# A two-layer expert kernel: early buffers for the first gather, context rows inside expert 0, the last two experts combined on chip

## The chip, the cores and the metric

The kernel runs on one core of a Trainium2 chip. The metric is the device time of one execution in microseconds (us). Comparisons are made between runs on the same chip; the profile is one execution, recorded instruction by instruction.

The engines go by short names: PE (TensorE, matrix products), DVE (VectorE), ACT (ScalarE), POOL (GpSimd) and SP (SyncE, which issues most of the DMA transfers). POOL issues the indirect transfers (gather and scatter by row numbers). All transfers share 16 DMA engines.

## The reference

512 latent tokens and 128 context tokens of width 1024 go through two layers with shared weights. All numbers are 32-bit floats. Each layer is:

```
h   = x * (1 + scale1) + shift1
mix = [windowed attention | neighbourhood attention | retention](h @ w_in) @ w_out
x   = layernorm(alpha * x + gate1 * mix)
h   = x * (1 + scale2) + shift2
aff = softmax(h @ w_router)                      # 16 experts
gate, idx = top_k(aff.T, cap)                    # each expert picks its tokens: 64 latent, 16 context
y_e = (silu(h[idx] @ w_gate) * (h[idx] @ w_up)) @ w_down * gate
ff  = scatter-add of the y_e of all experts to their tokens
x   = layernorm(alpha * x + gate2 * ff)
```

Latent and context tokens choose separately. So each expert works on 80 rows, and reads 8 MB of gate and up weights and 4 MB of down weights for them.

## The kernel before, in words

**Memory.** SBUF is handed out in 25 slots of 128 x 2048 floats (`Slots`), some cut into two halves (`Halves`). A 1 MB weight tile fills one slot. `ahead` is a list of all weight tiles in the order of use; `ahead.fill(n, keep)` issues loads as long as more than `keep` slots are free in the order of the program. A load into a slot whose last user still runs waits for it. Instructions are put in order on each engine by a planner, from costs that it assumes and from the order of the program; `tc.issue_after(x)` adds that an instruction stands behind `x` on its engine.

**From the mixer to the experts (`mixer`).** The output projection runs in two halves of 512 columns over five tiles of 128 tokens (tiles 0 to 3 latent, 4 context). Beside it `router(t)` computes the affinities of a tile and stores the normalized rows to DRAM (`znd`). Then `topk` (L1330 and following) finds the 64 best latent tokens of each expert in rounds of eight on DVE, merging two halves; `picked` (L1553) is the cast of the latent row numbers. After it on DVE come the gated output, the router and the top-k of the context tile (L1556 to L1566).

**The experts (`moe`).** `gather(0)` fetches the first expert's latent rows and context rows in two transfers, `gather(e)` the others two experts ahead, into three buffers `xgb`. `first_x` turns expert 0's rows with PE; `turned_x` and `turned_act` turn the other rows and the activations on DVE in 32 x 32 pieces (L1611). In `gate_up` the latent rows are the stationary operand, four column groups at a time (`lat`, L1681), and the context rows follow (`cxt`, L1685). For expert 0 all eight tiles run their latent products first, then all context products, and only these give the tiles' slots back. `down(e-1)` comes after `gate_up(e)`. It scales the result (L1739, L1746) and adds it to `acc` in DRAM by a scatter on POOL (L1754). `init` (L1455 to L1457) computes the start values of `acc`, `z * (alpha g) + alpha b`, on DVE and stores them.

**The end of a layer.** Expert 15's result isn't scattered. The sums are loaded from `acc` (L1814) after expert 14's scatter, and `combine` adds them up in PSUM: identity times sums (L1832, L1834) plus a 0/1 matrix times the result in two parts, high and low (L1835, L1836). `ln2` normalizes (L608, L1882) and, in layer 1, scales and shifts (L1884, L1885) and stores; in layer 0 it loads the tables and first weights of layer 1 after the sums, and starts layer 1's first projection.

Lines of the code that the steps turn on:

```
hf.hold = True
xgb = [hf.get(F32, "xg") for _ in range(3)]
xgs = [gather(0)]
init(6, g_last[0])
...
yh, yl = down(NE - 1, turned_act(prev))
for t in range(NT):
    sums = nc.sync.dma_start(accs[t], acc[l][128 * t:128 * t + 128])
```

## Time and profile before

| what | us |
|---|---|
| median of 3 runs (lowest to highest) | 1949.7 (1946.35 to 1953.62) |
| the profiled execution | 1953.35 |
| its span, first to last instruction | 1951.6 |
| PE busy | 1807.9 (93%) |
| DVE busy | 1151.8 (59%) |
| ACT busy | 417.7 (21%) |
| POOL busy | 224.5 (12%) |

The two expert passes take 440 to 964 us and 1390 to 1913 us of the span. PE is busy in nearly all of both, but a busy PE is not a PE at its peak: matmuls overlap, and their clock has two levels, 1.2 and 2.4 GHz. The granted clock is given as a share of the higher one.

### The profile page before, as it was taken

The page shows a single profiled execution, that of the slowest core. Times are in us where ns is not written, and L with a number is a line of the kernel's source. Part 1 is how long each engine was busy: PE and PEld are TensorE (multiplying, and loading weights), DVE is VectorE, ACT ScalarE, POOL GpSimd, SP SyncE. Part 2 cuts the span into 40 slices and gives each one's busy share as a digit, 9 for nine tenths or more (in the row PEclk, how much of TensorE's full clock was granted, in tenths as well). Part 3 has the DMA queues.
Part 4 walks back from the last instruction along what each step waited for, and adds up shares of the span by engine and source line. Part 5 has one row for each costly group of instructions (what it writes and reads, how often), then busy time and mean ns, then how long its engine had stood idle before and what let it go on. Part 6 is the DMA issues. An engine that isn't in the chain of part 4 may idle for free. (4 is left out here: it accounts for less than half of the span.)

```text
span 1951.6 us, 34372 instructions
## 1 busy us (share of the span) xinstructions
PE 1807.9 (93%) x14135; PEld 903.2 (46%) x14135; DVE 1151.8 (59%) x2966; ACT 417.7 (21%) x886; POOL 224.5 (12%) x176
## 2 busy tenths in 40 slices
PE   6999999868999999989879999989699999998995
PEld 3766767752333333323357667878223333332322
DVE  3654547568556585636386554675884657655356
ACT  2354533111000000000054654322100000000001
POOL 3200002101000110000062000130100101000003
PEclk9999999878999999999989999999699999999997
DMA  9343554488999999999545342247799999999973
GB/s 367 114 147 132 190 166 167 137 304 302 400 392 406 391 397 386 408 416 409 210 157 188 130 145 99 86 159 251 272 398 400 404 392 394 400 392 408 409 315 136
DMA packets 95980, 555.00 MB, mean 284 GB/s; under 512 B 13850, under 2 KB 18864, under 8 KB 36432
## 3 DMA queue, kind: packets, MB, share of 16 engines
q1 hardware_dynamic: 89104, 528.27, 68.9%
q0 software_dynamic: 6720, 24.54, 5.0%
q8 instruction: 111, 1.82, 0.4%
q14 instruction: 45, 0.37, 0.1%
HBM read 526.07 MB, written 26.70 MB: 283 GB/s over the span
## 5 line engine op out<-in xcount | busy, mean ns | idle before, releaser
L1681 PE MATMUL pA<-w,xT 128*32 128x512 f32 x4096 | 494.9, 605 | 24.3 <-DVE xT L1628 11.7
L1681 PEld LDWEIGHTS pA<-w,xT 128*32 128x32 f32 x4096 | 134.3, 112 | 340.6 <-issue 301.0
L1685 PE MATMUL pA<-w,xT 128*32 128x512 f32 x2048 | 270.0, 603 | 3.0 <-DVE xT L1652 3.0
L1681 PE MATMUL pB<-w,aT 128*32 128x512 f32 x2048 | 246.6, 598 | 5.7 <-issue 5.6
L1611 DVE STREAM_TRANSPOSE aT<-z 32x128 f32<-32x128 f32 x432 | 130.2, 301 | 53.2 <-PE pB L1681 27.6
L1681 PEld LDWEIGHTS pB<-w,aT 128*32 128x32 f32 x2048 | 69.9, 111 | 161.5 <-issue 146.6
L1685 PEld LDWEIGHTS pA<-w,xT 128*32 128x32 f32 x2048 | 68.1, 112 | 158.9 <-issue 153.3
L1685 PE MATMUL pB<-w,aT 128*32 128x512 f32 x1024 | 133.3, 593 | 0.0
L1611 DVE STREAM_TRANSPOSE aT<-turn 32x128 f32<-32x128 f32 x336 | 101.4, 302 | 25.3 <-PE pB L1681 19.4
L1715 DVE TENSOR_TENSOR z<-z,pA 128x512 f32<-128x512 f32 x18 | 12.4, 688 | 174.7 <-PE pA L1681 139.9
L348 PE MATMUL pA<-hhi,wh 128*128 128x512 f32 x224 | 92.1, 411 | 0.0
L1713 ACT ACTIVATE z<-pA 128x512 f32<-128x512 f32 x18 | 10.8, 598 | 376.6 <-PE pA L1681 376.6
L350 PE MATMUL pA<-hhi,wl 128*128 128x512 f32 x224 | 88.3, 396 | 0.5 <-DVE wl L345 0.5
L349 PE MATMUL pA<-hlo,wh 128*128 128x512 f32 x224 | 88.3, 394 | 0.0
L1685 PEld LDWEIGHTS pB<-w,aT 128*32 128x32 f32 x1024 | 35.6, 111 | 76.8 <-issue 75.0
L345 DVE TENSOR_TENSOR wl<-w,wh 128x1024 fp32r<-128x1024 f32 (+2 forms) x46 | 57.6, 1286 | 21.9 <-ACT wh L344 14.3
L348 PE MATMUL pA<-wh,cs 128*128 128x512 f32 x160 | 68.1, 428 | 1.9 <-ACT cs L344 1.9
L1713 ACT ACTIVATE turn<-pA 128x512 f32<-128x512 f32 x14 | 8.4, 597 | 274.3 <-PE pA L1681 274.3
L344 ACT ACTIVATE wh<-w 128x1024 fp32r<-128x1024 f32 (+2 forms) x50 | 53.8, 1121 | 51.9 <-DMA w<-win 29.3
L350 PE MATMUL pA<-wh,cs 128*128 128x512 f32 x160 | 64.2, 405 | 0.0
L349 PE MATMUL pA<-wl,cs 128*128 128x512 f32 x160 | 64.1, 401 | 0.0
L1754 POOL DMA_INDIRECT acc<-z,idx x16 | 23.5, 1466 | 343.6 <-DVE z L1746 326.8
(517 smaller groups left out, 2948.5 us busy)
## 6 DMA issues: line engine op xcount, KB each, us to landing
w<-wgu SPq DMA_DIRECT2D x256, 1024.0 KB, 19.9
w<-wdn SPq DMA_DIRECT2D x124, 1024.0 KB, 21.4
wada<-wada SPq DMA_DIRECT2D x48, 1024.0 KB, 5.0
w<-win SPq DMA_DIRECT2D x20, 1024.0 KB, 7.1
w<-wout SPq DMA_DIRECT2D x8, 1024.0 KB, 4.8
znd<-z SPq DMA_DIRECT2D x8, 512.0 KB
w<-wdn POOLq DMA_DIRECT2D x4, 1024.0 KB, 5.6
acc<-z SPq DMA_DIRECT2D x8, 512.0 KB, 3.3
```

Source lines behind the costliest of these rows:

```text
L344: hi_op[:] = [S.activation(hi[s], src[s], AF.Copy)]
L345: lo_op[:] = [E.tensor_tensor(lo[s], src[s], f32(hi[s]), op=ALU.subtract)]
L348: T.matmul(out, lh, rh, start=first, stop=False)
L349: T.matmul(out, lh, rl, start=False, stop=False)
L350: T.matmul(out, ll, rh, start=False, stop=last)
L1611: V.transpose(out, rows.rearrange("p (k q f) -> p k q f", q=4, f=32)[:, :, q, :])
L1681: T.matmul(p[32 * g:32 * g + 32], x[:, 64 * ko + 32 * i:64 * ko + 32 * i + 32], w[:, 512 * n:512 * n + 512], start=(ko == 0), stop=(ko == 7))
L1685: T.matmul(p[32 * g:32 * g + 32], x[:, 512 + 32 * ko:544 + 32 * ko], w, start=first, stop=last)
L1713: S.activation(act[:, 0:512], pl[0], AF.Silu)
L1715: V.tensor_mul(act[:, 0:512], act[:, 0:512], pl[1])
L1754: G.indirect_dma_start(out=acc[l], out_offset=IndirectOffsetOnAxis(ap=idx[:, e:e + 1], axis=0), in_=y[0:CAP, 0:1024], in_offset=None, comp ...
```

## The change

Six things change.

1. Expert 0's buffers (`early`: the turned rows and the three gather buffers) are taken and cleared in the mixer, before the second half of the output projection. The gather of the latent rows is issued behind `picked`; the context tile's top-k and places are put behind the latent part of `first_x` on DVE (`ctx_places`), and its rows are turned before the eighth latent tile of expert 0 instead of after it.
2. The `acc` start values of tiles 0 and 1 are computed on POOL before the top-k, those of tiles 2 to 4 on DVE after expert 0's activation. The rows `alpha g`, `alpha b` are loaded one tile later and scaled after the router of tile 3.
3. `kept_busy(22)`: 22 products of 256 columns with the identity on PE behind the output projection, whose result nobody reads.
4. Experts 14 and 15 are both kept on chip (`on_chip`), stacked in 128 rows for the latent tokens and 64 for the context tokens; the 0/1 matrix grows to match. Expert 15's activation is turned into a buffer of its own, before expert 14's down.
5. The sums are loaded right behind the last weights and one weight tile of the next layer; the first weight split of the next layer and the identity products of two tiles' sums stand before the last result.
6. `KQ` goes from 5 to 2 (free slots kept back from the weights up to expert 13), `NQ` from 2 to 0 (weight loads issued on POOL's queue).

```diff
-NQ = 2
+NQ = 0
-IW = 1
+IW = 2
-KQ = 5
+KQ = 2
...
+        def init(ts, E, after=None):
+            for i, op in ((0, ALU.mult), (1, ALU.add)):
+                for t in ts:
+                    z = zs[t]
+                    if after is not None:
+                        with tc.issue_after(after):
+                            E.tensor_tensor(z, z, agb[0][:, 1024 * i:1024 * i + 1024], op=op)
+                    else:
+                        E.tensor_tensor(z, z, agb[0][:, 1024 * i:1024 * i + 1024], op=op)
+                    if i:
+                        st(acc[l][128 * t:128 * t + 128], z)
+                        hf.free(z)
+            if NT - 1 in ts:
+                sl.free(*agb)
...
+        def scale_rows():
+            with tc.issue_after(e_last[0]):
+                for i in range(2):
+                    S.activation(agb[0][:, 1024 * i:1024 * i + 1024], agb[0][:, 1024 * i:1024 * i + 1024], AF.Copy,
+                                 scale=ALPHA)
+        def kept_busy(n):
+            p = psA()
+            with tc.issue_after(o_last[0]):
+                for _ in range(n):
+                    T.matmul(p[:, 0:256], ident, cst[:, 0:256], start=True, stop=True)
...
+        early = sl.get(F32, "xT"), [hf.get(F32, "xg") for _ in range(3)]
...
         drain(run_all(PY, o=ctx_out(), z=router(3)))
+        scale_rows()
+        kept_busy(22)
...
         ahead.fill(99, KO)
+        init((0, 1), G)
         topk(affT[:, 0:256], affT2, CAPL, cand[:, 0], cand[:, 1], cst[0:32, C_OFF:C_OFF + 1])
...
+        def ctx_places(after):
+            with tc.issue_after(after):
+                topk(affT[0:16, 256:384], affT2[0:16, 0:128], CAPC, selc[0:16, 0, 0:CAPC], selc[0:16, 1, 0:CAPC],
+                     float(NLAT))
+                for x in (1, 0):
+                    V.transpose(gsel[64:96, x, :], selc[:, x, :])
+                V.tensor_copy(idxC, gsel[CAPL:CAP, 1, 0:16])
+                V.tensor_copy(idx[CAPL:CAP], gsel[CAPL:CAP, 1, 0:16])
...
+                if e == 0 and ko == 7:
+                    next(first)
                 for q in range(2):
                     lat(pl[q], xT, w[:, 1024 * q:1024 * q + 1024], ko)
...
+            with tc.issue_after(x_last[2] if e else t_last[0]):
+                act_mul[:] = [V.tensor_mul(act[:, 0:512], act[:, 0:512], pl[1]).ins]
...
+        def on_chip(i, e, pl, pc, y):
+            if i == 0:
+                for x in "LC":
+                    yk[x] = hf.get(F32R, "yh"), hf.get(F32R, "yl")
+            o, q = slice(64 * i, 64 * i + 64), slice(32 * i, 32 * i + 32)
+            (Lh, Ll), (Ch, Cl) = yk["L"], yk["C"]
+            for n in range(2):
+                r, c = slice(64 * n, 64 * n + 64), slice(512 * n, 512 * n + 512)
+                st_ = lambda: V.scalar_tensor_tensor(y[o, c], pl[r], gateL[r, e:e + 1], g2[r, 0:512],
+                                                     op0=ALU.mult, op1=ALU.mult)
+                with tc.issue_after((lo_op[0] if i and l + 1 < DEPTH else sq_last[0]).ins):
+                    st_()
+                S.activation(Lh[o, c], y[o, c], AF.Copy)
+            for n in range(2):
+                c = slice(512 * n, 512 * n + 512)
+                lo = V.tensor_tensor(Ll[o, c], y[o, c], f32(Lh[o, c]), op=ALU.subtract)
...
-        xgs = [gather(0)]
-        init(6, g_last[0])
+        first_gather(slice(0, CAPL), znd[l][0:NLAT], idx)
+        xgs = [xgb[0]]
...
         xT, prev = next(first), None
+        ctx_places(x_last[1])
+        first_gather(slice(CAPL, CAP), znd[l], idxC)
...
-            init(7, x_last[1])
+            if e == 0:
+                init((2, 3, 4), V, act_mul[0])
+            if e == NE - 1:
+                left = len(ahead.todo)
+                if l + 1 < DEPTH:
+                    ahead_layer(l + 1)
+                rest = ahead.todo[left + 1:]
+                del ahead.todo[left + 1:]
+                ahead.fill(99, 3)
+                hf.free(*xgb)
+                accs.extend([hf.get(F32, "acc") for _ in range(NT)])
+                for t in range(NT):
+                    sums = nc.sync.dma_start(accs[t], acc[l][128 * t:128 * t + 128])
+                last_aT = turned_act(act, hf.get(F32, "aT"))
...
+        with tc.issue_after(sums.ins):
+            ahead.fill(KF, 4)
+            if l + 1 < DEPTH:
+                ahead.have.insert(0, ahead.have.pop(4))
+                first_ws[l + 1] = first_w(l + 1)
+            down(NE - 1, last_aT)
...
+        begin(0)
+        begin(1)
         return combine, sums.ins
```

`begin(t)` issues a tile's identity products, and `combine(t)` the two others.

## Rows read from the trace of the kernel before

**Rows 1.** Stretches of pass 1: length, busy per engine (instructions), PE clock, DMA share, GB/s.

```profile
1370.00:1380.00 10.00, 2.56 (x12) 2.30 (x12) 9.16 (x35) 1.12 (x2) 0.29 (x1) 0.50 0.97 404
1380.00:1390.00 10.00, 3.95 (x22) 3.68 (x21) 5.91 (x30) 2.42 (x7) 2.12 (x4) 0.50 0.53 184
1390.00:1400.00 10.00, 9.82 (x68) 2.51 (x72) 9.55 (x12) 0.58 (x2) 3.44 (x3) 0.73 0.28 74
1400.00:1410.00 10.00, 8.50 (x80) 2.62 (x76) 7.03 (x11) 2.90 (x6) 0.90 (x1) 0.95 0.95 358
...
1430.00:1790.00 360.00, 360.00 (x3360) 109.01 (x3356) 221.13 (x551) 27.75 (x47) 27.68 (x21) 1.00 1.02 399
...
1880.00:1910.00 30.00, 27.18 (x237) 8.95 (x232) 12.29 (x31) 2.38 (x4) 0.99 (x1) 0.94 0.38 152
```

**Rows 2.** Timeline of PE: start, length, operation, count, idle before and its releaser.

```profile
1377.44 1.94 PE L1385 MATMUL pC<-cst,catB 128*128 128x128 f32 x8 [11.89 <-issue]
1379.27 3.59 PE L1393 MATMUL pB<-m,work 128*128 128x16 f32 x16
1388.16 1.08 PE L1648 MATMUL pC<-cst,aT 64*128 64x64 f32 x8 [5.30 <-DMA aT<-znd,idx]
1390.18 16.46 PE L1681 MATMUL pA<-w,xT 128*32 128x512 f32 x128 [0.94 <-DVE xT L1652]
...
1408.74 8.77 PE L1685 MATMUL pA<-w,xT 128*32 128x512 f32 x64 [1.50 <-DVE xT L1652]
1422.21 7.05 PE L1681 MATMUL pA<-w,xT 128*32 128x512 f32 x48 [4.70 <-DVE xT L1628]
```

**Rows 3.** DMA issues from 1405 to 1900: count, size each, median us to landing.

```profile
w<-wgu SPq DMA_DIRECT2D x112, 1024.0 KB, 20.4
w<-wdn SPq DMA_DIRECT2D x62, 1024.0 KB, 21.7
```

**Rows 4.** Timeline of PE at the end of pass 1.

```profile
1886.88 1.90 PE L1681 MATMUL pB<-w,aT 128*32 128x512 f32 x16
...
1900.18 9.08 PE L1681 MATMUL pB<-w,aT 128*32 128x512 f32 x60 [2.82 <-issue]
...
1917.86 2.08 PE L1834 MATMUL pA<-z,cst 128*128 128x512 f32 x2 [4.71 <-DMA z<-acc]
```

**Rows 5.** Timeline there: DVE's scaling of expert 14, and POOL's scatter.

```profile
1896.57 1.51 DVE L1739 SCALAR_TENSOR_TENSOR catB<-pB,gateL,catB 64x512 f32<-64x512 f32 x2 [9.56 <-PE pB L1681]
...
1909.01 1.40 POOL L1754 DMA_INDIRECT acc<-catB,idx  x1 [33.18 <-DVE catB L1746]
```

**Rows 6.** Timeline of the tail: first statistics on DVE, first product on POOL.

```profile
1920.83 0.70 DVE L608 BATCH_NORM_STATS2 bs<-pA 128x6 f32<-128x512 f32 x1 [2.36 <-PE pA L1836]
...
1926.45 2.50 POOL L1884 TENSOR_TENSOR z<-z,ln 128x512 f32<-128x512 f32 x2 [1.28 <-ACT z L1882]
```

**Rows 7.** Timeline of the seam after layer 0: PE and ACT.

```profile
968.86 2.07 PE L1834 MATMUL pA<-z,cst 128*128 128x512 f32 x2 [4.62 <-DMA z<-acc]
...
980.09 1.45 ACT L1882 ACTIVATE z<-pA,nmr,rs 128x512 f32<-128x512 f32 x2 [2.44 <-DMA ln<-ln2b]
```

**Rows 8.** Timeline of DVE at the start of pass 1.

```profile
1375.38 0.17 DVE L1553 CAST idx<-gsel 64x16 int32<-64x16 f32 x1
...
1392.94 4.63 DVE L1455 TENSOR_TENSOR z<-z,lngb 128x1024 f32<-128x1024 f32 x4
...
1408.60 5.38 DVE L1611 STREAM_TRANSPOSE turn<-xg 32x256 f32<-32x256 f32 x12
```

**Rows 9.** Timeline of POOL there: the first gather.

```profile
1383.68 1.01 POOL L1590 DMA_INDIRECT aT<-znd,idx  x1 [3.43 <-PE pB L1393]
```

**Rows 10.** Timeline of ACT: the exponent of the last latent tile's router.

```profile
1360.86 0.31 ACT L1430 ACTIVATE ex<-m,rmx 128x16 f32<-128x16 f32 x1 [2.65 <-DVE rmx L1428]
```

**Rows 11.** Timeline of DVE and POOL beside each other in layer 0's seam.

```profile
1026.54 2.42 DVE L743 COPY z<-z 128x128 f32<-128x128 f32 x1
...
1026.15 2.72 POOL L1905 TENSOR_TENSOR acc<-acc,ln 128x1024 f32<-128x1024 f32 x1
```

More of the change, by code (lines that the diff above doesn't have):

```diff
@@ L349, in mm3 @@
         T.matmul(out, lh, rl, start=False, stop=False)
-        T.matmul(out, ll, rh, start=False, stop=last)
+        return T.matmul(out, ll, rh, start=False, stop=last).ins
     def mm3x2(pairs):
@@ L1514, in mixer @@
             less_work()
+        early = sl.get(F32, "xT"), [hf.get(F32, "xg") for _ in range(3)]
+        for i in range(2):
+            G.memset(early[0][:, 1024 * i + 512:1024 * i + 768], 0.0)
+        for x in early[1]:
+            G.memset(x[64:96], 0.0)
         wo += [weights(AH_P, KP, E=G if WO[2 + i] == "1" else V) for i in range(2)]
@@ L1603, in ld_after @@
                 G.dma_start(out, in_)
-        xTs = sl.get(F32, "xT")
+        xTs, xgb = early
         aTs = hf.get(F32, "aT")
         bufs = [xTs[:, 0:768], xTs[:, 1024:1792]]
+        sq_last = []
         def squares(out, rows, q):
-            V.transpose(out, rows.rearrange("p (k q f) -> p k q f", q=4, f=32)[:, :, q, :])
+            sq_last[:] = [V.transpose(out, rows.rearrange("p (k q f) -> p k q f", q=4, f=32)[:, :, q, :])]
         def turned_x(src):
@@ L1736, in down @@
                 sl.free(w)
+            y = hf.get(F32, "y")
+            if last >= 0:
+                on_chip(last, e, pl, pc, y)
+                return
             for n in range(2):
@@ L1748, in down @@
             hf.free(tC)
-            if last:
-                split(yy[0][0:CAP], yy[1][0:CAP], y[0:CAP])
-                sl.free(xTs)
-                hf.free(y, aTs)
-                return yy
             G.indirect_dma_start(out=acc[l], out_offset=IndirectOffsetOnAxis(ap=idx[:, e:e + 1], axis=0),
@@ L1756, in down @@
             hf.free(y)
+        def on_chip(i, e, pl, pc, y):
[14 more added lines that the diff above has]
+                lo = V.tensor_tensor(Ll[o, c], y[o, c], f32(Lh[o, c]), op=ALU.subtract)
+            hf.free(y)
+            tC, yc = hf.get(F32, "yC"), hf.get(F32, "yc")
+            S.activation(tC[0:64, 0:512], pc[64:128], AF.Copy)
+            with tc.issue_after(lo.ins):
+                V.tensor_tensor(tC[0:64, 512:1024], pc[0:64], tC[0:64, 0:512], op=ALU.add)
+                for n in range(2):
+                    r = slice(32 * n, 32 * n + 32)
+                    V.scalar_tensor_tensor(yc[q, 512 * n:512 * n + 512], tC[r, 512:1024], gateC[r, e:e + 1],
+                                           g2[r, 512:1024], op0=ALU.mult, op1=ALU.mult)
+                split(Ch[q], Cl[q], yc[q])
+            hf.free(tC, yc)
+        yk = {}
         def keep(e):
             return KL if e >= 14 else KQ
-        accs, hot = [], []
+        accs, hot, act_mul = [], [], []
         def places():
             hot.append(hf.get(F32, "iota"))
-            ld(hot[0][0:CAP, 0:NTOK],
-               bass.AP(tensor=a["iota"].tensor, offset=a["iota"].offset, ap=[[0, CAP], [1, NTOK]]))
+            ld(hot[0][:, 0:NTOK], bass.AP(tensor=a["iota"].tensor, offset=a["iota"].offset, ap=[[0, 128], [1, NTOK]]))
         def one_hot():
@@ L1801, in moe @@
             prev = act
-        hf.free(*xgb)
         hf.release()
-        if AA == 1:
-            accs.extend([hf.get(F32, "acc") for _ in range(NT)])
         open_work()
-        if AA == 2:
-            accs.extend([hf.get(F32, "acc") for _ in range(NT)])
-        ahead.fill(KF, 4)
-        yh, yl = down(NE - 1, turned_act(prev))
-        for t in range(NT):
-            if AA == 0:
-                accs.append(hf.get(F32, "acc"))
-            sums = (G if SQ == "G" else nc.sync).dma_start(accs[t], acc[l][128 * t:128 * t + 128])
-        hf.free(g2)
+        ahead.add(rest)
+        with tc.issue_after(sums.ins):
[4 more added lines that the diff above has]
+            down(NE - 1, last_aT)
+        sl.free(xTs)
+        hf.free(aTs, last_aT, g2)
+        (yh, yl), (ch, cl) = yk["L"], yk["C"]
         oh = hot[0]
@@ L1819, in moe, with begin @@
                 sl.free_ = sl.free_[-LF:] + sl.free_[:-LF]
-            if WB != 2:
-                ahead_layer(l + 1)
         c_last = []
+        sums_of = {}
+        def begin(t):
+            ps_ = sums_of[t] = []
+            for n in range(2):
+                p = {"A": psA, "B": psB, "C": psC}[(PB if l + 1 < DEPTH else P2)[t]]()
+                if c_last:
+                    with tc.issue_after(c_last[-1]):
+                        T.matmul(p, ident, accs[t][:, 512 * n:512 * n + 512], start=True, stop=False)
+                else:
+                    T.matmul(p, ident, accs[t][:, 512 * n:512 * n + 512], start=True, stop=False)
+                ps_.append(p)
@@ L1840, in combine @@
             if t == NT - 1:
-                hf.free(yh, yl, oh)
-            return ps_, accs[t]
+                hf.free(yh, yl, ch, cl, oh)
+            return sums_of[t], accs[t]
+        begin(0)
+        begin(1)
         return combine, sums.ins
-    first = {}
     def ln2(l, combine, sums):
```

116 lines of the change are left out of this document (45 added, 71 removed).

## The prediction, made before the result was known

> **What bounds the kernel now.** Read the stretches of the second expert pass first [rows 1]. From 1430 to 1790 us PE is busy all the time at the full clock, and so are the DMA engines (share 1.02): 3360 matmuls in 360 us are 0.107 us each, 2.57 us for the 24 of one 1 MB weight tile. Which of the two is the bound shows at the edges. Before the pass the DMA engines are full until just before 1380 and then nearly idle until 1400 (0.53, 0.28): every weight slot is full, and expert 0 gives none back before its context products run at 1408.74 [rows 2]. From 1400 they are full until about 1880 + 0.38 x 30 = 1891.4. In these 491.4 us they bring 112 + 62 tiles from SP [rows 3], one from POOL's queue (the second of its two) and five `acc` stores of half a tile: 177.5 tiles, so 2.77 us a tile with the gathers and scatters between them. That is slower than PE's 2.57. So the DMA engines limit the pass, and the 17 tiles loaded before it are PE's lead, which shrinks by 0.2 us a tile; each us that the engines rest before 1401 is lost for good.
>
> Then read the ends. Expert 15's down starts at 1900.18, after 2.82 us of idle [rows 4]: its activations are turned on DVE behind expert 14's scaling, which waited 9.56 us for PE [rows 5]. The sums can't be loaded before expert 14's scatter, issued at 1909.01 behind those transposes, has landed; PE waits 4.71 us for them, until 1917.86 [rows 4, 5]. I call the end of the last down product E: 1917.86 - 4.71 = 1913.15. The first statistics on the sums come at E + 7.7, the first POOL product at E + 13.3 [rows 6], and the span ends at E + 38.5. In layer 0 the same point is 968.86 - 4.62 = 964.24, and ScalarE's first normalization comes 15.85 us later, the last 2.44 us of its wait behind small loads issued after the sums [rows 7].
>
> **Part 1, the start of a pass (layer 1's times).** The latent places are cast at 1375.55 [rows 8], but the gather goes out at 1383.68, when PE's context router has let go of the memory that the gather buffer is given [rows 9]. Taken early, the buffer is free, and POOL can issue at 1375.6, if its four new products (two tiles, multiply and add) are done. They start after the exponent at 1360.86 and its read (1361.3) [rows 10] and one half of the row scaling (1.45, as two 512-column ACT passes take in [rows 7]): 1362.8. Four at 2.72 [rows 11] end at 1373.7. Margin 1.9 us. The two `acc` stores move to this idle DMA time; SP has nothing but small rows to issue then.
>
> These products run beside the top-k, and a DVE copy of 128 columns took 2.42 us behind a POOL product, where the POOL product of 2.72 ended [rows 11]. No row shows a MAX8 or FIND_INDEX8 beside POOL: between 0 and 10.9 us for all four products. I take 0, the margin keeping the copies and two-input operations at the end of the top-k clear. The Trainium skill, "SBUF — State Buffer", section "Who interferes with whom", says that a DVE instruction with at most one SBUF input, outside the two-port modes, does not contend with GpSimd, while copies and two-input ones wait for the whole GpSimd instruction. By that rule the top-k costs nothing and the picks up to 2.7 us if POOL runs late; the copy's row agrees with its second half.
>
> The gather took 4.5 us until PE ran on it [rows 2, 9]; beside the two stores I take 1381 (1380.1 to 1384.5). On PE the context router stands ahead; now it ends at 1379.27 + 3.59 = 1382.9 [rows 2]. Then 2.0 us from transposes to the first latent product [rows 2]: the pass starts at 1384.5 instead of 1390.18 (1383 to 1389).
>
> The 22 unread products cost PE time that is idle (it has nothing from 1365.6 to 1377.44 [rows 2]): a 512-column f32 product took 2.08 at half clock [rows 4], so 256 columns take 0.52 at the full clock, 11.5 us in all, just done at 1377. They keep the granted clock, which was 0.50 in 1370:1390 [rows 1], up until then; the context router and the gather wait follow with gaps. Expert 0's latent products took 16.46 [rows 2]; at 0.107 they are 13.8. I take 15.1. The context transposes (8, between 6 and 7 of 8 tiles) add 0.7 to PE, and what stands behind them, tile 7 and all context products, waits if the context gather is late. Its places come some 4 us after the latent xT and the gather takes 4.5, so by 1394, against 1398. Context products start at 1384.5 + 15.8 = 1400.3 instead of 1408.74 (1397.5 to 1406), the first slot is free at 1401.2. Expert 1's xT needs 8 transposes of 0.45 [rows 8] and more, about 7 us, beside the 6.9 us of context products: PE's 4.70 us wait [rows 2] all but goes.
>
> **What the DMA engines make of it.** The early pieces take two slots, so 14 instead of 16 tiles are loaded ahead; KQ=2 allows two more at the pass's first fill: 16 against 17. After the restart there are 176 tiles and three `acc` stores, 177.5 tiles again: 491.4 us from 1401.2, so 1892.6 (1889 to 1898), against 1891.4. So the nine us that PE wins at the start buy no DMA time. KQ=2 gives more slots to engines that are already full: 0. NQ=0 moves two loads from POOL to SP: 0. The new `acc` products on DVE (three tiles, 1.2 us each operation [rows 8]) and the larger one-hot lie in a pass where DVE is busy 221 of 360 us [rows 1].
>
> **Part 2, the end of a pass.** PE, its lead gone, follows the landings. Of the last eight tiles (experts 14 and 15 down) the first lands 8 x 1.4 to 8 x 2.77 before the end of the stream (half-way shared or strictly in turn): expert 15's gate and up then end near 1892.6 - 16.7 + 2.6 = 1878.5 (1873 to 1884), where PE now ended at 1886.88 [rows 4] because it stalled and ran cold in between. With its own buffer the last activation is turned beside expert 14's down (24 transposes against 10.3 us), and both downs follow without a gap: E = 1878.5 + 20.6 = 1899.1, 14.0 earlier (9 to 18). In each layer: 28.0.
>
> **Part 3, behind the last product.** With expert 14 kept on chip the sums wait for expert 13's scatter only and load behind the last weights, and two tiles' sums stand in PSUM before E. E to the first full sum: scaling 0.76 [rows 5], partly before E, ACT copy 0.73, subtract 0.7, products 0.4: E + 2 instead of E + 7.7. The two halves follow closer, so POOL starts at E + 5.7 instead of E + 13.3. From there DVE and POOL alternate over the scale and shift as now: 25.15 us to the span's end. Gain 7.6 (4 to 11). In layer 0 the small loads leave before E too, and the first weight split is done ahead; the first normalization comes at E + 4.8 instead of 15.85: 11.0 (5 to 16), the rest of the seam unchanged. Expert 14's context split adds some 3 us to a DVE that idles there.
>
> **Sum.** The profiled execution took 1953.35 (span 1951.6 and 1.75 around it). 28.0 + 7.6 + 11.0 = 46.6: 1906.7. The median of the runs is 3.65 below that execution: 1903 us. With every bound at its end the gain is 27 to 63: 1886 to 1923.
>
> **Rivals.** (a) The loads ahead are not ahead: SP is one queue, and a sum whose slot is still held by expert 15's weights blocks those behind it. For it: SP often waits for slots; against: the three gather buffers are free by then, which is three of the five halves. Only the 28 remain, less a little: 1922, chance 0.14. (b) The `acc` stores of tiles 2 to 4 stand on SP ahead of the first freed slots. They wait for DVE work put after expert 0's activation, until about 1415: the restart slips by 14, part 2 is lost, 18.6 remain: 1931. For it: one queue; against: the planner can put loads first that are ready first. 0.09. (c) Top-k and POOL block each other after all: up to 10 us, the start falls back to now's, 5.7 a layer: 1915, 0.07. (d) PE and not DMA limits the pass: E would be 1407 + 184 x 2.57 = 1880, 19 earlier still in each layer: 1865; the share of 1.02 speaks against it. 0.05. (e) The other side: with KQ=2 the halves for activations and outputs share two spare slots, and a load put in a slot that is freed late holds all of SP's queue. If the DMA engines rest u us in each of 32 experts, 1.46 us eat the whole gain, from 1.76 the kernel is slower by over 0.5%; at 2 us, 1967. Against it: the engines never rest with KQ=5, and slots return every 2.6 us. 0.08.
>
> My forecast has 0.57. Its own range is 1888 to 1921; to the other cases, 1885 to 1932. Within 0.5% (10 us, about what a measurement of this kernel can tell from no change): 0.06, from mixtures of (b) and (e); slower 0.08; faster 0.86.
>
> **What would show it.** The gather issued near 1375.6 and the first latent product near 1384.5; DMA share back at 1 near 1401, with no long gap in it later; PE stalls of some tenths a tile in the second half of a pass; expert 15's down right behind 14's; `acc` loads issued before E; the first statistics about 2 us behind E. Wrong if the DMA engines rest after 1401, or if E moves by under 9 us.

## The result and the profile after

The changed kernel takes 1926.5 us (median of 4 runs, 1925.8 to 1927.4) by 1949.8 for the kernel before: a ratio of 0.988, 95% interval 0.986 to 0.990. That is 23.3 us, half of the 46.6 forecast. The time lies 3.5 us above the forecast's own range (1886 to 1923) and inside the wider one that takes in the rivals (1885 to 1932). The profiled executions differ by 26.7 (spans 1951.6 and 1924.9), because that of before was some 3.6 us above its median.

To see which steps gave it, cut both spans at four marks: the first MAX8 of each layer's top-k (412.92 and 1362.64 before, 411.58 and 1343.31 after), E (the end of the last down product: 964.24 and 1913.15, now 957.44 and 1889.69), ScalarE's first normalization behind E in layer 0, and the end.

| stretch | before | after | gain | forecast |
|---|---|---|---|---|
| start to first MAX8, layer 0 | 412.9 | 411.6 | 1.3 | 0 |
| MAX8 to E, layer 0 | 551.3 | 545.9 | 5.5 | 14.0 |
| E to first normalization | 15.85 | 10.59 | 5.3 | 11.0 |
| from there to MAX8, layer 1 | 382.6 | 375.3 | 7.3 | 0 |
| MAX8 to E, layer 1 | 550.5 | 546.4 | 4.1 | 14.0 |
| E to the end | 38.45 | 35.21 | 3.2 | 7.6 |

**The start of a pass** went as forecast on PE. Chosen rows of the changed kernel's timeline, layer 1 (start, length, engine and line, operation, what ended the idle time before):

```profile
1342.95 9.36 POOL L1459 TENSOR_TENSOR z<-z,lngb 128x1024 f32<-128x1024 f32 x4 [6.75 <-ACT lngb L1477]
1343.31 0.42 DVE L1338 MAX8 m<-m 32x8 f32<-32x256 f32 x1
...
1355.77 0.17 DVE L1578 CAST idx<-gsel 64x16 int32<-64x16 f32 x1
1356.22 1.00 POOL L1617 DMA_INDIRECT xg<-znd,idx  x1 [3.90 <-DVE idx L1578]
1359.90 2.60 PE L1395 MATMUL pB<-m,work 128*128 128x16 f32 x16
1364.36 1.09 PE L1679 MATMUL pC<-cst,xg 64*128 64x64 f32 x8 [1.86 <-DMA xg<-znd,idx]
1366.12 14.76 PE L1710 MATMUL pA<-w,xT 128*32 128x512 f32 x112 [0.67 <-DVE xT L1683]
...
1383.14 7.05 PE L1714 MATMUL pA<-w,xT 128*32 128x512 f32 x64
```

The gather goes out 0.4 us behind its cast, 12.9 us behind the first MAX8 (it was 21.0) [rows 9]; the latent products start at MAX8 + 22.8 (27.5; forecast 21.9), the context products at MAX8 + 39.8 (46.1; forecast 37.7) [rows 2]; expert 1 follows without the 4.70 us wait. POOL's four products stand right beside the top-k, and a MAX8 still takes 0.42 us, as it did without them.

The stretches of this pass (length, busy us and instructions of PE, its weight loads, DVE, ACT, POOL, then PE clock, DMA share, GB/s):

```profile
1360.00:1370.00 10.00, 7.47 (x44) 4.31 (x48) 6.78 (x36) 3.43 (x8) 0.57 (x1) 0.55 1.03 370
1370.00:1380.00 10.00, 10.00 (x92) 2.74 (x88) 0.00 (x0) 0.00 (x0) 2.74 (x3) 0.94 0.88 331
1380.00:1390.00 10.00, 10.00 (x100) 3.20 (x92) 8.43 (x21) 3.01 (x6) 2.12 (x2) 1.00 0.61 222
...
1430.00:1790.00 360.00, 341.77 (x3132) 124.57 (x3128) 213.56 (x525) 26.06 (x44) 23.58 (x19) 0.97 1.02 401
1650.00:1680.00 30.00, 27.71 (x248) 8.10 (x244) 10.02 (x23) 0.60 (x1) 0.00 (x0) 0.94 1.01 409
...
1710.00:1740.00 30.00, 22.75 (x176) 7.08 (x179) 19.73 (x47) 1.08 (x2) 3.80 (x3) 0.79 1.02 385
1880.00:1910.00 30.00, 23.95 (x132) 10.60 (x124) 24.55 (x43) 10.51 (x15) 10.10 (x10) 0.95 0.05 18
```

Two things are to be seen. The DMA engines now rest (0.12 + 0.39) x 10 = 5.1 us at the start of the pass; before it was (0.03 + 0.47 + 0.72 + 0.05) x 10 = 12.7 [rows 1]. And PE, which before was busy for all of 1430 to 1790 with 3360 products, does 3132 now: it stands still around 1650 to 1725, and the clock falls there, while the DMA engines stay full.

**Where PE stands.** Its waits in layer 1's pass (who waited for whom: us, times, longest), and PE's timeline there and at the end:

```profile
PE pB L1714 <- DVE g L1642: 7.8, 1, 7.8
PE pB L1710 <- DMA w<-wdn: 5.8, 1, 5.8
PE pA L1710 <- DMA w<-wgu: 4.7, 2, 2.4
```

```profile
1642.63 3.62 PE L1714 MATMUL pB<-w,g 128*32 128x512 f32 x32
1648.62 1.92 PE L1710 MATMUL pA<-w,xT 128*32 128x512 f32 x16 [2.37 <-DMA w<-wgu]
...
1653.69 2.82 PE L1710 MATMUL pA<-w,xT 128*32 128x512 f32 x16 [2.29 <-DMA w<-wgu]
...
1700.04 3.64 PE L1710 MATMUL pB<-w,g 128*32 128x512 f32 x32
1711.48 5.87 PE L1714 MATMUL pB<-w,g 128*32 128x512 f32 x32 [7.80 <-DVE g L1642]
1723.12 1.93 PE L1710 MATMUL pB<-w,g 128*32 128x512 f32 x8 [5.77 <-DMA w<-wdn]
...
1868.87 1.93 PE L1710 MATMUL pB<-w,g 128*32 128x512 f32 x16
...
1888.61 1.08 PE L1714 MATMUL pA<-w,xg 128*32 128x512 f32 x8
1889.62 1.98 PE L1908 MATMUL pA<-xg,cst 128*128 128x512 f32 x4
```

At 1648 and 1653 PE waits for gate and up tiles that have not landed: there its lead is gone, as forecast. At 1711 it waits with products of a down (L1714, context rows) whose activations DVE has not turned yet, and at 1723 for a down tile. These two are work that the planner put ahead of later gate and up tiles (e3, below, takes them away by order alone). After it PE has no wait again. PE's stock of tiles can be estimated: tiles that have landed (a load counts as landed 21.7 us after its issue, the median here, where its landing isn't recorded) less PE's products divided by 24. It is 1.5 at 1640, 9 at 1740, and about 7 (6.8 to 7.7) from 1760 to 1860. At the end it is far behind the DMA engines, as SP's queue shows (the last weights, then the first sums; first of the kernel before, then of the changed one):

```profile
1856.06 17.71 SPq L289 DMA_DIRECT2D w<-wdn  x8
```

```profile
1830.11 18.93 SPq L289 DMA_DIRECT2D w<-wdn  x8
1864.05 0.33 SPq L1873 DMA_DIRECT2D xg<-acc  x1
```

The last of these loads goes out 0.33 us before the end of its row: at 1848.71, MAX8 + 505.4 (before 1873.44, MAX8 + 510.8). Loads here took 20.3 us in the median to land, so the last weights were there at 1869.0. At 1868.87 PE only began expert 14's down, with all eight down tiles in hand: 8 x 2.57 = 20.6 us to E.

**The end.** Chosen rows of the changed kernel's timeline, ScalarE in layer 0's seam, then the tail:

```profile
968.03 1.45 ACT L1967 ACTIVATE xg<-pA,nmr,rs 128x512 f32<-128x512 f32 x2 [4.35 <-DVE nmr L616]
...
1891.44 1.88 PE L1908 MATMUL pB<-catB,cst 128*128 128x512 f32 x4
1894.54 1.30 DVE L610 BATCH_NORM_STATS2 bs<-pA 128x6 f32<-128x512 f32 x2
1895.75 1.28 DVE L610 BATCH_NORM_STATS2 bs<-pB 128x6 f32<-128x512 f32 x2
1897.06 1.22 DVE L345 TENSOR_TENSOR yl<-z,yl 32x1024 fp32r<-32x1024 f32 x1
1898.31 0.28 DVE L612 BATCH_NORM_AGGREGATE mv<-bs 128x2 f32<-128x12 f32 x2
1901.02 2.50 POOL L1969 TENSOR_TENSOR xg<-xg,ln 128x512 f32<-128x512 f32 x2 [1.03 <-ACT xg L1967]
```

The first statistics come at E + 4.9 (before E + 7.7), POOL's first product at E + 11.3 (before E + 13.3) [rows 6]. The identity products of the sums stand behind E, not ahead of it (L1908, 3.7 us); and DVE does the second tile's statistics (pB) and the context split (L345) before it sums up the first tile's (L612).

### The profile page after: what moved, and what is told of

It reads as the page before. It is cut to its first block, busy times and chain, and to the rows that moved or that the text cites. A ratio compares the mean times of both kernels' runs of the same rounds, so it can differ in the third digit from the quotient of the medians.

```text
span 1924.9 us, 34546 instructions
## 1 busy us (share of the span) xinstructions
PE 1805.4 (94%) x14223; PEld 968.0 (50%) x14223; DVE 1137.3 (59%) x2968; ACT 425.3 (22%) x898; POOL 236.0 (12%) x188
## 4 chain that ended last, share of the span: by engine, by line
PE 59%; DMA 32%; DVE 5%; issue 2%; ACT 1%; POOL 0%; SPq 0%; DVEq 0%; ACTq 0%; POOLq 0%
DMA w<-wgu 20%; PE pA L1710 11%; DMA w<-wdn 10%; PE pA L348 7%; PE pA L350 6%; PE pA L349 6%; PE pA L1714 5%; PE pB L1710 5%; PE pB L356 3%; PE pB L1714 2%; PE pC L813 2%; PE pA L517 2%; PE pA L917 2%; PE pB L491 1%; PE pB L1395 1%
## 5 line engine op out<-in xcount | busy, mean ns | idle before, releaser
L1710 PE MATMUL pA<-w,xT 128*32 128x512 f32 x4096 | 512.0, 599 | 9.8 <-DMA w<-wgu 8.2
L1710 PEld LDWEIGHTS pA<-w,xT 128*32 128x32 f32 x4096 | 161.8, 111 | 295.9 <-issue 270.9
L1714 PE MATMUL pA<-w,xT 128*32 128x512 f32 x2048 | 288.7, 594 | 1.5 <-DVE z L1745 1.5
L1710 PE MATMUL pB<-w,g 128*32 128x512 f32 x1920 | 236.0, 599 | 13.6 <-DMA w<-wdn 13.6
L1714 PEld LDWEIGHTS pA<-w,xT 128*32 128x32 f32 x2048 | 82.6, 110 | 142.4 <-issue 141.0
L1710 PEld LDWEIGHTS pB<-w,g 128*32 128x32 f32 x1920 | 78.1, 111 | 145.3 <-issue 140.2
L1714 PE MATMUL pB<-w,g 128*32 128x512 f32 x960 | 130.1, 610 | 15.6 <-DVE g L1642 15.6
L1642 DVE STREAM_TRANSPOSE g<-z 32x128 f32<-32x128 f32 x384 | 116.1, 302 | 28.2 <-PE pB L1710 13.3
L1642 DVE STREAM_TRANSPOSE catB<-xg 32x256 f32<-32x256 f32 x240 | 104.3, 435 | 3.4
L1781 POOL DMA_INDIRECT acc<-catB,idx x22 | 31.3, 1422 | 461.4 <-DVE catB L1778 461.4
L1714 PEld LDWEIGHTS pB<-w,g 128*32 128x32 f32 x960 | 38.9, 113 | 84.3 <-issue 81.6
L1642 DVE STREAM_TRANSPOSE g<-xg 32x128 f32<-32x128 f32 x240 | 72.6, 302 | 12.7 <-PE pB L1710 9.1
L1623 POOL DMA_INDIRECT xg<-znd,idx x30 | 29.9, 997 | 322.7 <-DVE catB L1642 301.2
L345 DVE TENSOR_TENSOR wl<-w,wh 128x1024 fp32r<-128x1024 f32 (+2 forms) x46 | 54.5, 1220 | 20.4 <-ACT wh L344 12.8
L348 PE MATMUL pA<-wh,hhi 128*128 128x256 f32 x192 | 59.5, 312 | 5.7 <-ACT hhi L344 3.8
## 6 DMA issues: line engine op xcount, KB each, us to landing
w<-wgu SPq DMA_DIRECT2D x256, 1024.0 KB, 21.2
w<-wdn SPq DMA_DIRECT2D x128, 1024.0 KB, 21.9
```

Source lines behind the costliest of these rows:

```text
L345: lo_op[:] = [E.tensor_tensor(lo[s], src[s], f32(hi[s]), op=ALU.subtract)]
L348: T.matmul(out, lh, rh, start=first, stop=False)
L1642: sq_last[:] = [V.transpose(out, rows.rearrange("p (k q f) -> p k q f", q=4, f=32)[:, :, q, :])]
L1710: T.matmul(p[32 * g:32 * g + 32], x[:, 64 * ko + 32 * i:64 * ko + 32 * i + 32], w[:, 512 * n:512 * n + 512], start=(ko == 0), stop=(ko == 7))
L1714: T.matmul(p[32 * g:32 * g + 32], x[:, 512 + 32 * ko:544 + 32 * ko], w, start=first, stop=last)
L1781: G.indirect_dma_start(out=acc[l], out_offset=IndirectOffsetOnAxis(ap=idx[:, e:e + 1], axis=0), in_=y[0:CAP, 0:1024], in_offset=None, comp ...
```

## The experiments

Marks of every run, in us of its profiled execution. "Last issue" is the last weight load of layer 1's pass on SP.

| run | median | 95% of ratio to before | MAX8 to E, layer 0 | E to MAX8, layer 1 | MAX8 to last issue | MAX8 to E, layer 1 | E to end |
|---|---|---|---|---|---|---|---|
| before | 1949.8 | | 551.3 | 398.4 | 510.8 | 550.5 | 38.4 |
| after | 1926.5 | 0.986 to 0.990 | 545.9 | 385.9 | 505.4 | 546.4 | 35.2 |
| e1, start alone | 1936.7 | 0.991 to 0.995 | 549.3 | 389.9 | 506.4 | 549.2 | 37.3 |
| e2, end alone | 1924.6 | 0.984 to 0.989 | 543.8 | 385.2 | 511.6 | 547.2 | 35.1 |
| e3, PE in order | 1923.9 | 0.984 to 0.989 | 546.3 | 385.8 | 505.8 | 541.4 | 35.2 |
| e4, before in order | 1950.9 | 0.998 to 1.001 | 551.1 | 404.8 | 511.7 | 548.5 | 35.8 |
| e5, scaling first | 1934.4 | 0.990 to 0.993 | 542.6 | 397.9 | 505.7 | 544.0 | 35.3 |
| e6, sums before E | 1930.8 | 0.988 to 0.991 | 547.3 | 388.0 | 505.3 | 547.1 | 36.0 |
| e7, KQ=5, NQ=2 | 1930.0 | 0.988 to 0.991 | 547.8 | 387.3 | 506.3 | 548.1 | 35.1 |
| e8, nothing unread | 1930.6 | 0.989 to 0.992 | 547.5 | 386.8 | 506.0 | 546.6 | 35.2 |
| e9, one scaling, layer 1 | 1912.8 | 0.979 to 0.983 | 547.1 | 385.8 | 506.5 | 530.8 | 35.2 |
| e10, fewer transfers | 1900.8 | 0.974 to 0.977 | 547.1 | 384.4 | 482.4 | 521.3 | 34.0 |
| e11, both layers | 1914.4 | 0.981 to 0.985 | 541.0 | 387.3 | 504.7 | 536.7 | 35.2 |
| e12, end alone in order | 1928.0 | 0.987 to 0.992 | 545.4 | 386.4 | 510.6 | 548.4 | 35.1 |

Runs e1 to e8 were made on one chip and e9 to e12 on another, each beside runs of the kernel before (medians 1949.8 and 1949.9 on the first, 1951.1 and 1947.8 on the second). So a difference between e9 and e3 compares two chips; but up to the edit of e9 their instructions stand in the same order, and there their stretches agree to 0.8 us. "E to MAX8, layer 1" holds the seam and the mixer of layer 1.

**e1 and e2: the two halves apart.** e1 is the changed kernel with the end of a layer as before (expert 14 scattered, `combine` with expert 15 alone, sums loaded after expert 14's scatter). e2 is the kernel before with the new end:

```diff
+            if e == NE - 1:
...
+                accs.extend([hf.get(F32, "acc") for _ in range(NT)])
+                for t in range(NT):
+                    sums = nc.sync.dma_start(accs[t], acc[l][128 * t:128 * t + 128])
+                last_aT = turned_act(act, hf.get(F32, "aT"))
```

> The start of a pass alone (parts 1 to 3 and 6 of the change, with the end of a layer as in the kernel before). The prediction's step says that PE's earlier start buys no DMA time and so nothing at the end of a pass: within 1945 to 1955 us. Rival: the 6 us that PE starts earlier reach the end of each pass: 1934 to 1940 us. Second rival: the two slots taken early cost lead, PE runs dry sooner and stalls longer: 1955 to 1965 us.

> The end of a layer alone (two experts on chip, own buffer for the last activation, sums ahead) on the kernel before. As the prediction has it this edit earns all of the gain: 14.0 a layer at the last product, 7.6 and 11.0 behind it, 1903 us. Rival, from the profile after: PE had landed tiles in hand at the end of its pass, so the last product moves only by the 2.8 us of idle time of the kernel before and some of the scaling, and what is behind it gives 12.5 and 3.2: 1926 to 1934 us.

The end alone gives as much as the whole change, the start alone 13 us, and together they give no more than the end. e2's 1924.6 lies 22 us above what the prediction's step gives and 1.4 below its rival's range. e1's time is the one that its first rival named, but not for its reason: E moved by 2.0 and 1.3 us, and 8.5 of the 13 lie between E and layer 1's MAX8. What e1 shows of the start is the last issue: 4.4 us sooner, though no part of the end was changed.

**e3 and e4: PE in the order of the program.** Each expert product is put behind the one before it in the source, in the changed kernel (e3) and in the kernel before (e4):

```diff
+        def in_row(*args, **kw):
+            with tc.issue_after(pe_row[0]) if pe_row else nullcontext():
+                pe_row[:] = [T.matmul(*args, **kw).ins]
...
-                    T.matmul(p[32 * g:32 * g + 32], x[:, 64 * ko + 32 * i:64 * ko + 32 * i + 32],
+                    in_row(p[32 * g:32 * g + 32], x[:, 64 * ko + 32 * i:64 * ko + 32 * i + 32],
```

> The changed kernel with all expert products on PE in the order of the program, that is of the loads. Theory A (order): PE's stall of 19 us in the middle of a pass comes from down products that stand ahead of the gate and up products whose weights are loaded first; in order the waits shrink to what the DMA engines are late by, PE ends 3 to 10 us behind the last landing instead of 20, and each pass is 10 to 17 us shorter: 1893 to 1907 us. Theory B (rate): PE must give back what the engines are slower by, in whatever order: 1921 to 1931 us. Theory C (clock): in order there are many small waits, PE falls to 1.2 GHz between them, and half of the gain is lost: 1908 to 1918 us.

> The kernel before with all expert products on PE in the order of the program. Theory A (order): its stall of 5.3 us and cold products around 1790 us, after which five landed tiles stay in hand, go in part: 5 to 10 us a pass, 1930 to 1940 us. Theory B (rate): no change, 1945 to 1955 us. Theory C (clock): waits spread over the pass and PE runs at 1.2 GHz more often than now: 1950 to 1965 us.

By the totals both are theory B (in e4 the range of theory C holds too), and theory A looked dead. The trace of e3 says otherwise: the stall in the middle is gone, and one of 8.0 us stands before expert 14's down in its place. PE, then DVE there:

```profile
1855.47 1.92 PE L1709 MATMUL pB<-w,g 128*32 128x512 f32 x16
1865.39 11.35 PE L1709 MATMUL pB<-w,g 128*32 128x512 f32 x80 [8.00 <-DVE catB L1777]
```

```profile
1854.78 0.69 DVE L1751 TENSOR_TENSOR z<-z,pA 128x512 f32<-128x512 f32 x1 [16.19 <-PE pA L1709]
1855.50 5.05 DVE L1642 STREAM_TRANSPOSE xg<-z 32x128 f32<-32x128 f32 x16
...
1863.82 1.51 DVE L1777 SCALAR_TENSOR_TENSOR catB<-pB,gateL,g 64x512 f32<-64x512 f32 x2
```

Expert 14's down needs the PSUM that expert 13's scaling (L1777) gives back. DVE stood idle for 16.19 us with that scaling ready, but the planner had put it behind the product for expert 15's activation (L1751), which waited for PE, and behind 24 transposes. In the kernel before (e4) layer 1's pass got 2.0 us shorter and the stretch ahead of it 6.4 us longer: in all no change.

**e5 and e9: that scaling first.** e5 does it for all experts and both layers, but only for the first of the two products of the activation. e9 does it for expert 15 of layer 1 alone, there for both products. The diff is that of e9, against the changed kernel; beside it both have e3's edit:

```diff
-            with tc.issue_after(x_last[2] if e else t_last[0]):
+            with tc.issue_after(scaled[0] if l and e == NE - 1 else x_last[2] if e else t_last[0]):
                 act_mul[:] = [V.tensor_mul(act[:, 0:512], act[:, 0:512], pl[1]).ins]
...
-            V.tensor_mul(act[0:64, 512:1024], act[0:64, 512:1024], up[0:64, 0:512])
+            with tc.issue_after(scaled[0]) if l and e == NE - 1 else nullcontext():
+                V.tensor_mul(act[0:64, 512:1024], act[0:64, 512:1024], up[0:64, 0:512])
...
-                V.scalar_tensor_tensor(y[CAPL:CAP, 512 * n:512 * n + 512], tC[r, 512:1024], gateC[r, e:e + 1],
-                                       g2[r, 512:1024], op0=ALU.mult, op1=ALU.mult)
+                scaled[:] = [V.scalar_tensor_tensor(y[CAPL:CAP, 512 * n:512 * n + 512], tC[r, 512:1024],
+                                                    gateC[r, e:e + 1], g2[r, 512:1024], op0=ALU.mult, op1=ALU.mult).ins]
```

> The changed kernel with PE's expert products in program order, and DVE's scaling of an expert's result put ahead of the product for the activation two experts on. In the run with PE's order alone one stall of 8.0 us a layer was left, at expert 14's down: its PSUM is given back by the scaling of expert 13, which had been ready 26 us before but stood on DVE behind a product that waited for expert 15's gate and up. Theory A (order of the two engines): that stall goes, nothing takes its place, 8 us a layer: 1906 to 1913 us. Theory B (rate of the DMA engines): PE then waits for landings instead, 0 to 2 us a layer: 1919 to 1927 us.

> The changed kernel with PE's expert products in program order (the run e3), and in layer 1 alone DVE's scaling of expert 13 put ahead of the two products for expert 15's activation. PE's order is that of e3 everywhere, and DVE's up to the end of layer 1, so only that place differs. Theory A (order of DVE): the stall of 8.0 us before expert 14's down in layer 1 goes and E comes 6 to 8 us sooner there: 1916 to 1918 us by e3's 1923.9. Theory B (rate): the tiles of expert 14's down have only just landed, PE waits for them instead, E moves by 0 to 3 us: 1921 to 1924 us.

e5 missed both ranges, theory A's by 21 us. Layer 0's pass did get shorter (542.6 by 546.3), though 4.4 us of the stall stayed, since the second product for the activation was still ahead. But from E to layer 1's MAX8, where the source is that of e3, it took 12 us more: the planner puts the whole program in order, and with other times in layer 0 it chose another order there. PE's longest wait in 1150 to 1228 in e5, where e3's longest is 0.4 us:

```profile
PE pB L348 <- DVE mx L1034: 3.9, 1, 3.9
```

This wait is 4 us of it; PE also was at 0.59 and 0.72 of its clock in 1215 to 1225, and the rest I have not followed. e9 avoids this by leaving layer 0 alone: PE's order is that of e3 everywhere, and DVE's differs only at the place of the edit. PE, DVE and SP of e9 at the end of layer 1's pass:

```profile
1854.91 10.51 PE L1709 MATMUL pB<-w,g 128*32 128x512 f32 x96 [0.17 <-DMA w<-wdn]
1865.21 10.51 PE L1709 MATMUL pA<-w,xg 128*32 128x512 f32 x96
```

```profile
1837.75 1.50 DVE L1778 SCALAR_TENSOR_TENSOR catB<-pB,gateL,g 64x512 f32<-64x512 f32 x2
...
1854.01 0.69 DVE L1751 TENSOR_TENSOR z<-z,pA 128x512 f32<-128x512 f32 x1 [13.22 <-PE pA L1709]
```

```profile
1830.59 21.13 SPq L289 DMA_DIRECT2D w<-wdn  x8
```

The scaling stands 16 us ahead of the product, the 8.0 are gone, and E comes 10.6 us sooner in layer 1 (530.8 by 541.4), more than the stall and more than theory A's 6 to 8; the total is 11.1 lower. E = 1875.72 is 24.3 us behind the last issue; in the changed kernel it was 41.0. A landing of some 21.7 us (the median in this run) and a last tile of 2.57 make these 24.3: here the landings set the end, as the prediction had it, and PE runs out of stock just as the last tile lands (its only wait for one is the 0.17 us above). Theory A holds for PE and DVE taken together, in layer 1.

**e10: do the DMA engines set the pace?**

```diff
             xg = xgb[e % 3]
+            if l and 4 <= e < 12:
+                return xg
...
-            G.indirect_dma_start(out=acc[l], out_offset=IndirectOffsetOnAxis(ap=idx[:, e:e + 1], axis=0),
-                                 in_=y[0:CAP, 0:1024], in_offset=None, compute_op=ALU.add)
+            if not (l and 3 <= e < 11):
+                G.indirect_dma_start(out=acc[l], out_offset=IndirectOffsetOnAxis(ap=idx[:, e:e + 1], axis=0),
+                                     in_=y[0:CAP, 0:1024], in_offset=None, compute_op=ALU.add)
```

> As the run before it (e9), and in layer 1 the gathers of experts 4 to 11 and the scatters of experts 3 to 10 are left out (the rows of earlier experts are used again, and those results are not added). That takes some 8 times 2.7 us off the DMA engines (their queue was busy 2.7 us in 40 us, a little over one expert, in the second pass of the kernel before) and nothing off PE or DVE. If the DMA engines set the pace of the pass: the last weights are issued some 20 us sooner, PE is bound by its own 2.57 us a tile and E comes 6 to 15 us sooner than in e9. If the waits for DVE set it: the last weights come sooner and E by 0 to 3 us.

They set the pace of the loads. The same stretch of the pass in e9, then in e10, and what PE waits for most in e9's pass (us, times, longest):

```profile
1430.00:1790.00 360.00, 353.18 (x3276) 119.04 (x3272) 216.81 (x533) 25.79 (x44) 25.34 (x20) 1.00 1.02 401
```

```profile
1430.00:1790.00 360.00, 360.00 (x3360) 132.17 (x3356) 224.56 (x553) 27.89 (x47) 10.40 (x8) 1.00 1.02 413
```

```profile
PE pB L1709 <- DVE catB L1778: 3.7, 2, 1.9
...
PE pB L1709 <- DVE g L1642: 2.7, 1, 2.7
```

The last weights are issued 24.1 us sooner, which shows that the engines pace the stream of loads. PE has no wait in this stretch, and E comes 9.5 sooner, now 38.9 behind the last issue: PE's own rate is the bound there. The 9.5 took two things. DVE's order differs in part from e9's from the start of the pass on (the planner again), so e9's waits for DVE are gone: 84 products more by 1790 are 9.0 of the 9.5. And with e9's landings PE could not have used them, since there the last tile landed just in time. So e10 does not show what fewer transfers alone would give at E.

**e6: the sums ahead of E.** On e5, the first two tiles' identity products are pinned ahead of the last weight tile's products:

```diff
+                if last == 1 and k == 3:
+                    with tc.issue_after(pe_row[0]):
+                        begin(0)
+                        begin(1)
+                    pe_row[:] = [b_last[0]]
```

> As the run before, and the identity products of the first two tiles' sums pinned ahead of the last weight tile's products, as the prediction had assumed that they stand. They took 3.7 us behind the last down product in the changed kernel. If they are what keeps the first statistics at E + 4.9 instead of E + 2: 2.5 to 3.7 us less in each layer, 5 to 7 us below the run before. If the scaling and the split of the last result are as late: 0 to 2 us below it.

Its place, PE and DVE:

```profile
1888.49 1.98 PE L1838 MATMUL pA<-xg,cst 128*128 128x512 f32 x4
...
1892.12 2.78 PE L1709 MATMUL pA<-w,xg 128*32 128x512 f32 x24
1894.12 1.53 DVE L1806 SCALAR_TENSOR_TENSOR z<-pA,gateL,g 64x512 f32<-64x512 f32 x2 [6.37 <-PE pA L1709]
...
1898.15 1.28 DVE L610 BATCH_NORM_STATS2 bs<-pA 128x6 f32<-128x512 f32 x2
```

The first statistics come at E + 3.25 by 4.89, but the products take PE 3.6 us there (1888.49 to 1892.12) and E itself comes 3.1 us later, since PE has no idle time before it: from MAX8 the statistics come at 550.4 by 548.9 in e5. The 3.6 us by which e6's total is below e5's come from a mixer 9.9 us shorter. The assumption of the prediction's part 3 was wrong twice: the products don't stand ahead of E, and they would earn nothing there.

**e7 and e8: the two small edits undone in the changed kernel.** e7: `KQ = 5`, `NQ = 2`. e8: the line `kept_busy(22)` is removed.

> The changed kernel with KQ back at 5 and NQ back at 2. The prediction gave both nothing, as the DMA engines are full whatever slots are free: 1922 to 1931 us. Rival: with three slots fewer for weights in the first half of a pass PE's lead at the restart is smaller by up to three tiles of 0.2 to 2.6 us: 1928 to 1940 us. Rival on the other side: the shared spare halves cost time with KQ=2, and 5 gains: 1910 to 1920 us.

> The changed kernel without the products whose result nobody reads. They ran while PE had nothing else, and the granted clock fell to 0.55 behind them all the same before expert 0's products. If the clock is what they were worth: expert 0's products take 16.5 us again instead of 14.7, some 2 us a layer that the DMA engines then hide or not: 1926 to 1931 us. If they are worth nothing: 1924 to 1929 us.

e7 is 3.5 us above the changed kernel and e8 4, with intervals that overlap its own (0.986 to 0.990); layer 1's last issue is within 1 us in both. So by the medians none of the three edits is worth more than some 4 us, and neither run names a cause. e8 lies in the range of its first case, but not for its reason, which rested on a misreading: 14.7 us are 112 products of the changed kernel, 16.5 are 128 of the kernel before, whose first 112 took 14.74 as well. In e8 the pass starts 1.5 us later behind MAX8 (PE's context router runs at 0.50 of the clock and takes 3.60 us for 2.60), and the first latent products take less, not more:

```profile
1364.86 3.60 PE L1395 MATMUL pB<-m,work 128*128 128x16 f32 x16
1372.07 14.05 PE L1709 MATMUL pA<-w,xT 128*32 128x512 f32 x112 [2.58 <-DVE xT L1682]
```

**e11 and e12: what the runs pointed to.** e11 has e9's edit in both layers and e6's in layer 0. e12 has e3's and e9's edits on e2, that is without the early gather.

> The version that the runs point to: PE's expert products in program order, the scaling of expert 13 ahead of expert 15's activation in both layers, and in layer 0 the identity products of two tiles ahead of the last weight tile's (with them the order of layer 1's mixer is that of the run e6, 2 us longer than in e9; without them it is that of e5, 12 us longer). If layer 0's last product moves as layer 1's did in e9, 10.6 us sooner: 1912.8 - 10.6 + 2 = 1904, 1901 to 1908 us. Rival: what is gained there is lost in the mixer again: 1911 to 1916 us.

> The end of a layer alone (as in e2, with the start of a pass as in the kernel before), PE's expert products in program order, and in layer 1 expert 13's scaling ahead of expert 15's activation as in e9. From the first MAX8 of layer 1's top-k to the last weight issue it took 511 us with the start of before and 505 to 506 with that of after. If the landings set the end of the pass in this kernel as in e9 (24.3 us behind the last issue), the last product comes 535 to 537 us behind that MAX8, by 530.8 in e9: the start is worth 5 us a layer once nothing else waits. If the prediction was right that the start buys no DMA time: 530 to 532. In all, with layer 0 as it falls: 1912 to 1930 us.

e11's layer 0 got 6.1 us shorter (10.6 expected), but with the other times there the planner ordered DVE differently in layer 1's pass, which took 536.7 by e9's 530.8: 1914.4, no better than e9. That is the rival's time, but the loss is in the pass and not in the mixer (387.3 by 385.8 from E to MAX8). e12's total lies in its range, but on the start it answers neither way: E came 37.8 us behind the last issue there, so the landings were not what set it, and what the start is worth at E is shown by no run. The best version that does all the work stays e9: 1912.8 us, 0.981 of the kernel before.

## Why the prediction came out half right

The bound and the start on PE were right. Of the gain, 28.0 us were to come from the last product of each pass, and there the prediction failed by its own sign ("wrong if E moves by under 9 us"): E moved by 5.5 and 4.1. That the time still lies inside the wider range is in part luck: 8.6 of the 26.7 us came in stretches forecast as unchanged, and neither rival that made the range so wide, (a) or (b), took place.

- **The bound** was named rightly. The DMA engines are full through the pass in every run, and taking 16 small transfers away moved the last weights by 24.1 us (e10).
- **The start of a pass, on PE:** right to some 2 us in each place named. Only the 15.1 us for expert 0's latent products failed: the clock was back at 0.50 when they began, in spite of the unread products, and the first 112 took 14.76 us by 14.74 before. Rival (c) fell: MAX8 and its kin (MATCH_REPLACE8, FIND_INDEX8) took 0.37 to 0.42 us beside POOL's products, as they did without them in the kernel before. That agrees with the rule of the Trainium skill, "SBUF — State Buffer", section "Who interferes with whom": one SBUF input, no contention.
- **The start, on the DMA engines:** wrong. The step "the nine us that PE wins at the start buy no DMA time" counted the same rest of the engines and the same number of tiles after it. The engines rested 5.1 us instead of 12.7: two `acc` stores and four loads, issued 11.6 to 24.9 us behind MAX8, fill what was idle, and the weights start again at MAX8 + 40.9 instead of + 42.2. The last weights went out 7.3 us (layer 0) and 5.4 (layer 1) sooner behind MAX8. e1 shows it with the start alone; every run without the new start has 510.6 to 511.7 in layer 1, every one with it (but e10) 504.7 to 506.5.
- **The end of a pass** is the step that failed: "PE, its lead gone, follows the landings", 14.0 us a layer. It measured 5.5 and 4.1. PE's lead did run out, at 1648, but it did not stay so: PE then stood 13.6 us on products put ahead of their turn, lost clock behind it, and took up a stock of tiles in that time that it still had at the end: eight landed and unread when the last one landed. I had read the kernel before as limited by the landings up to its end, though there too E came 39.7 us behind the last issue (24.3 in e9), and PE's stock, by the same estimate, went from 1.8 tiles at 1780 to 4.6 at 1820. In e9, with the order of PE and DVE mended in layer 1, E came 530.8 us behind MAX8, where the forecast put it at 1899.1 - 1362.6 = 536.5. So the mechanism was there to be had, and an order worked out from assumed costs hid it: 15.6 us of it in that layer (5.0 by e3, 10.6 by e9). For layer 0 no run shows as much; the shortest pass there is e11's 541.0.
- **Own buffer for the last activation, two experts kept:** right. Expert 15's down follows 14's without a gap, and the sums are loaded from 1864.05, 25.6 us before E; rival (a) fell.
- **Behind the last product:** 3.2 instead of 7.6, for the two reasons shown at e6 and the order on DVE in the tail (statistics of the second tile and a split ahead of the first tile's sum). Right was that the wait for the sums goes.
- **The seam of layer 0:** 11.0 forecast, 5.3 measured up to the first normalization, by the same lateness; then 7.3 from there to MAX8, the rest of the seam and the mixer, that I had as unchanged. e1 has these 7.3 without the new end, e2 has 8.0 with the mixer's source as before, and with that source unchanged too e4 lost 10.1 there, e5 12.1 by e3. So I put it down to the planner's order; that is argued, not shown. In e2 some 6 of the 8.0 lie in the seam, in the changed kernel most of the 7.3 in the last 300 us ahead of MAX8. Which instructions give it stays open.
- **KQ, NQ, rivals (b), (d), (e):** KQ and NQ gave nothing that the runs can tell from no change, as forecast. The `acc` stores of (b) went out at 1399 to 1402 between loads; SP's queue stood 6.2 us for the first of them, but the DMA share stayed at 1.01 to 1.02 from 1390 on, and the engines never rested behind the restart, which settles (e) too. (d) fell: E was not 19 us earlier.

So the sum, for the profiled executions: 46.6 - 18.4 (E in the two layers) - 5.7 (seam) - 4.4 (tail) + 8.6 (the two stretches up to MAX8) = 26.7 us.

## What to carry to other kernels

Where a planner fixes the order of engines from costs that it assumes, an edit moves not only its own place: cut the span at marks and compare each stretch, or a gain in one hides a loss in another (e5 and e11). When a stream of loads is the bound, look how far behind the last landing the last product ends; here it was 20.7 us, eight landed tiles; PE's products in the order of the loads gave back 5.0 us, and one scaling put ahead on DVE 10.6 more. An instruction that is ready but stands behind one that waits costs nothing in any list of costly groups: look for an idle engine whose next instruction waits while a later one could run.

## What the runs showed of the hardware

- A stall costs more than its length. The 32 context products behind the 7.8 us wait took 5.87 us, where 32 of the same kind took 3.62 at the full clock (at 1642.63); the granted clock of 1710 to 1740 was 0.79. Taking away the 8.0 us of stall in e3 brought 10.6: the 80 products behind it had taken 11.35 us, where 96 took 10.51 without it.
- With the DMA engines full, a 1 MB load takes 20 to 22 us to land (medians of 20.4 and 21.7 before [rows 3], 22.0 and 21.7 in e9, 21.2 in e10), and SP issues one about every 2.5 to 3 us, so seven or eight are on their way at a time.
- Gathers and scatters of 80 rows cost these engines more than their bytes: POOL's queue had 8.0% of their time for 7.5 MB in 1410 to 1800 of e9 and 2.8% for 2.6 MB in e10, 20 us for eight pairs, about 2.5 us a pair of 0.6 MB, about as long as a whole weight tile of 1 MB. The queue's packets, MB and share in e9, then in e10:

```profile
q0 software_dynamic: 2208, 7.54, 8.0%
```

```profile
q0 software_dynamic: 768, 2.62, 2.8%
```
